# Sums of squares folded in transposed 32-blocks, factors kept as one row in memory, latents' factors spread by a product, gates run one group later

## The chip, the cores and the metric

The kernel runs on one core of a Trainium2 chip. The metric is device time in microseconds (us) of one execution. Engines are named as the profile names them: PE (TensorE, matmuls), DVE (VectorE), ACT (ScalarE), POOL (GpSimd) and SP (SyncE, which only issues DMAs here). PE, DVE, ACT and POOL each run their instructions strictly in the order in which the compiler lists them.

## The reference, cut to what matters

Two layers over 512 tokens and 2048 features, all in float32. One input projection feeds three mixers and a gate for each of their 16 heads; two places in the mixers divide by a root mean square over features, and these are what the change touches: the latents of the first mixer and the heads of the differential mixer.

```python
def rms_norm(x, g):
    y = x * lax.rsqrt(jnp.mean(x * x, axis=-1, keepdims=True) + NORM_EPS)
    return y * g

def mla_mixer(c_q, c_kv, k_rope, pos, q_norm_g, kv_norm_g, w_uq, w_ukv):
    q = (rms_norm(c_q, q_norm_g) @ w_uq)        # c_q: 384 features ("cq")
    kv = (rms_norm(c_kv, kv_norm_g) @ w_ukv)    # c_kv: 256 features ("ckv")
    ...
def diff_mixer(q, k, v, pos, lam, lam_init, subln_g):      # 5 heads of 128 features
    pr = softmax(q1 k1) - lam * softmax(q2 k2)
    o = rms_norm(pr @ v, subln_g) * (1.0 - lam_init)
    ...
for i in range(DEPTH):                                      # DEPTH = 2
    z = rms_norm(h, norm_g[i]) @ w_in[i]
    o_a, o_b, o_c = mla_mixer(...), dsa_mixer(...), diff_mixer(...)     # 6, 5 and 5 heads
    h = h + concat(o_a * silu(g_a), o_b * silu(g_b), o_c * silu(g_c)) @ w_o[i]
    h = h + (p[i] @ w_ple[i]) * sigmoid(h @ w_pg[i])
return rms_norm(h, final_g)
```

## The kernel before

Activations lie transposed: features on the 128 partitions, the 512 tokens on the free axis, one tile of 128x512 for each 128 features (pool name "g", 59 buffers, `slot()`). A float32 matrix product is made of two halves of each operand, high and low, in a type that TensorE takes at one column rate (`split_into`, L258: ACT copies the high half, L260, DVE subtracts it from the source, L261), and of three products (`mm3`, L356, lines L358 to L360).

**The input projection** runs through 15 groups (`IN_GROUPS`), each of up to four output tiles of 128 features. A group goes through 8 chunks of weights (DMA by SP into "wr", split into "wh" and "wl", 4 buffers each), with 24 matmuls a chunk, and sums in four accumulators in PSUM (pool "pp", 4 banks, so that the next group can begin only in those banks that have been emptied). When a group ends, `take` empties its banks: for queries and keys by an ACT copy (L633), for gates by a DVE product with the factors R (L629) and a silu on ACT (L630). What it writes to are "raw" tiles (pool name "z", 8 buffers for all).

**The mixers** run as a side stream (`mixers`): between two steps of the projection `pump` lets the stream go on by as much PE time as its share allows; a `yield` with a number books the PE time of what was just issued. `heads` runs first the five heads of the differential mixer (c0 to c4), then the five of the sparse mixer: scores (L364, L365), softmax (L547, L548 and behind them L815, L816), transposes of the probabilities (L564), their split into "th" and "tl" (L260, L261), the product with the values (the twelve matmuls of one `attend`), for c heads the squares of the result (L821), and a copy (L644) which POOL sends to memory (L646). A head's query and key raw tiles come free when `rope` has read them, which is done for the next head behind the one at hand.

The groups that the prediction speaks of: group 6 makes gates ga0, ga1 and qc1, kc1 (query and key of head c1); group 7 qc2, kc2, qc3, kc3; group 8 ga2, ga3, qc4, kc4; group 9 qb0, kb0, qb1, kb1; group 10 ga4, ga5, qb2, kb2; group 11 qb3, kb3, gc0, gc1; groups 12 to 14 hold the other gc and all gb gates.

**Norms.** `col_sums` (L308) turns the sum over the 128 partitions into four float32 matmuls with the data as weights and two columns of ones as the moving side (L313), so that each token's sum stands in a partition of its own; `rsqrt` works on these columns; `spread` (L330) brings them back, by four transposes of a broadcast column (L334), to a 128x512 tile whose rows are all alike. `latents` (L650) uses both (two calls a layer), `diff_after` (L825) sums for each c head into "csum", and `gate` (L900) spreads csum for each gc head.

**Gates.** At the end of each group the main loop (L949 to L953) takes all its tiles and then runs `gate` for its gates: load of the head's output from memory (SP, L905), product with the silu of the raw tile (DVE, L911 for ga and gb, L909 for gc). The raw tile of a gate is held until this product.

The scheduler places the instructions of all streams on their engines ahead of time; the list of each engine is fixed in the program.

Of the kernel before, what the change touches and what calls it, by code (L numbers as in the profile page):

```python
# [198 lines left out]
def trunk(ctx: ExitStack, tc: tile.TileContext, t, out):  # L199
# [53 lines left out]
    identb = const.tile([128, 128], BF16, name="identb")  # L253
    DVE.tensor_copy(identb, identf)
    onesf = const.tile([128, 2], F32, name="onesf")
    DVE.memset(onesf, 1.0)
# [47 lines left out]

    mean = const.tile([128, 4 * C_H], F32, name="mean")
    corr = const.tile([128, 4 * C_H], F32, name="corr")

# [7 lines left out]

    def rsqrt(dst, src, n, size):

        y, m, e = dst[:, :n], mean[:, :n], corr[:, :n]
        o = 0
        for x in src if isinstance(src, list) else [src]:  # L320
            DVE.tensor_scalar(mean[:, o:o + x.shape[1]], x, 1.0 / size, EPS, op0=ALU.mult, op1=ALU.add)
            o += x.shape[1]
        ACT.activation(y, m, AF.Sqrt)
        DVE.reciprocal(y, y)
        DVE.tensor_tensor(e, y, y, op=ALU.mult)
        DVE.tensor_tensor(e, e, m, op=ALU.mult)
        DVE.tensor_scalar(e, e, -0.5, 1.5, op0=ALU.mult, op1=ALU.add)
        DVE.tensor_tensor(y, y, e, op=ALU.mult)
# [256 lines left out]
    for L in range(DEPTH):  # L585
# [24 lines left out]
        def take(nm):  # L610
            nonlocal wi
            kind, j = nm
            if kind in ("vb", "vc", "v5"):
# [9 lines left out]
                if kind == "v5":  # L623
                    wi = const.tile([128, NB, 8], F32, name=f"wi{L}")
                    for b in range(NB):
                        DVE.tensor_scalar(wi[:, b], z[nm][b][:, 256:264], rcol[:, b:b + 1], None, op0=ALU.mult)
# [23 lines left out]
        def latents(kind, n, size, gain, res):  # L650
# [8 lines left out]
            yield GAP  # L659
            r = sm(4)  # L660
            rsqrt(r, col_sums(total), 4, size)
            yield 0.45
            yield GAP
            rb = spread(r)
            for j in range(n):
# [125 lines left out]

        csum = const.tile([128, 4 * C_H], F32, name=f"csum{L}")

# [31 lines left out]
        def diff_after(x, s):  # L825
            DVE.tensor_copy(csum[:, 4 * x:4 * x + 4], col_sums(s))
            yield 0.45
            if x == C_H - 1:
                rsqrt(csum, csum, 4 * C_H, 128)
                done.add(("csum", 0))  # L830

# [68 lines left out]
        def gate(kind, x):  # L900
            m = {"ga": 0, "gb": 6, "gc": 11}[kind] + x
            s = raw.pop((kind, x))
            finish(("out", m))
            o = slot()
            nc.sync.dma_start(o, odram[m])  # L905
            if kind == "gc":
                finish(("csum", 0))
                DVE.tensor_tensor(o, o, spread(csum[:, 4 * x:4 * x + 4]), op=ALU.mult)
                DVE.scalar_tensor_tensor(o, o, sub_c[:, L:L + 1], s, op0=ALU.mult, op1=ALU.mult)  # L909
            else:  # L910
                DVE.tensor_tensor(o, o, s, op=ALU.mult)  # L911
            gated[m] = o
# [11 lines left out]
        def mix(k):  # L924
            mix_until(k + 4)
            return mixed[k]

        fac = factors()
        main = Side(mixers(), SHARE)
        Side(choose(), 0.37)  # L930
        for gi, names in enumerate(IN_GROUPS):
# [4 lines left out]
            for got in gen:  # L936
                if gi == 0 and L == 0 and got == 2:
                    angles()
                if gi == 0 and L == 0 and got == 4:
                    lambdas()  # L940
                if gi == 0 and got in (5, 6):
                    next(fac)
                if gi == len(IN_GROUPS) - 1 and got in (3, 4, 5, 6):
                    mix_until(got - 2)
# [4 lines left out]
            for nm in names:  # L949
                take(nm)  # L950
            for nm in names:
                if nm[0] in ("ga", "gb", "gc"):
                    gate(*nm)  # L953
        if L == 0:
# [151 lines left out]
```

## Time and profile before

| what | us |
|---|---|
| median of 3 runs | 2294.86 (2294.57 to 2295.43) |
| the profiled execution | 2295.42 |
| its span in the trace | 2293.6 |
| PE busy | 2272.2 (99%) |
| DVE busy | 1366.9 (60%) |
| ACT busy | 1006.9 (44%) |
| POOL busy | 114.9 (5%) |

The mean granted clock of TensorE was 0.997 of full speed. The busy time of PE comes from ends that are modelled: a matmul overlaps the next one, so what one costs is read from the distance between two starts, not from its printed duration. Two more views are used: the timeline of an engine (start, duration, engine, line, operation, tiles, count, and in brackets the idle time ahead and what ended it) and a table of stretches of time with each engine's busy time and the granted clock.

### The profile page before, as it was taken

To read this page: it belongs to the slowest core of one execution; us is meant where nothing else is said; L and a number is where in the kernel's file an instruction comes from. 1 tells how busy PE (TensorE), PEld (TensorE's weight loads), DVE (VectorE), ACT (ScalarE), POOL (GpSimd) and SP (SyncE) were. 2 spreads that over 40 slices of the span, in tenths; PEclk is the share of its full clock that TensorE was granted. 3 is DMA by queue.
4 is the path that set the end of the run, shared out by engine and by line. 5 is a ranking of instruction groups with operands and counts; after the bars stand their busy time and mean duration, and the time that the engine had idled before them with its cause. 6 is when DMAs were issued, how large, how long until landed. Compare 5 with 4: busy or idle time off the path is not lost.

```text
span 2293.6 us, 29988 instructions
## 1 busy us (share of the span) xinstructions
PE 2272.2 (99%) x10988; PEld 1913.0 (83%) x10988; DVE 1366.9 (60%) x2886; ACT 1006.9 (44%) x1931; POOL 114.9 (5%) x204
## 2 busy tenths in 40 slices
PE   8999999999999999999999999999999999999997
PEld 7898888888888888888888888888888888888887
DVE  7655559977767543344555555699676665333445
ACT  6444445454545432233434444444554454223444
POOL 0000000000000011000000000000000000110003
PEclk9999999999999999999999999999999999999998
DMA  6233323323334345344332333233232243553235
GB/s 201 70 99 116 113 79 96 111 93 97 97 101 161 106 139 185 126 134 136 128 96 76 101 120 104 83 97 102 97 106 102 88 165 115 170 174 130 100 102 165
DMA packets 95220, 268.33 MB, mean 117 GB/s; under 512 B 10976, under 2 KB 26848, under 8 KB 95072
## 3 DMA queue, kind: packets, MB, share of 16 engines
q1 hardware_dynamic: 81760, 223.41, 30.5%
q0 software_dynamic: 13312, 43.00, 5.5%
q8 instruction: 86, 1.41, 0.3%
q14 instruction: 62, 0.51, 0.1%
HBM read 235.96 MB, written 30.41 MB: 116 GB/s over the span
## 4 chain that ended last, share of the span: by engine, by line
PE 98%; ACT 0%; issue 0%; DMA 0%; POOL 0%; SPq 0%; DVE 0%; POOLq 0%; ACTq 0%
PE pp L358 28%; PE pp L359 28%; PE pp L360 28%; PE at L360 3%; PE at L359 3%; PE at L358 3%; PE at L564 2%; PE at L365 1%; PE at L364 1%; PE at L313 1%; PE at L334 0%; DMA x<-in_x_dram 0%; PE at L853 0%; POOL g L1044 0%; ACT wh L260 0%
## 5 line engine op out<-in xcount | busy, mean ns | idle before, releaser
L261 DVE TENSOR_TENSOR wl<-wr,wh 128x512 fp32r<-128x512 f32 (+4 forms) x810 | 530.5, 660 | 731.4 <-ACT wh L260 671.2
L358 PE MATMUL pp<-g,wh 128*128 128x512 f32 (+1 forms) x2432 | 936.0, 386 | 6.2 <-ACT g L263 5.7
L359 PE MATMUL pp<-g,wh 128*128 128x512 f32 (+1 forms) x2432 | 936.1, 385 | 0.0
L260 ACT ACTIVATE wh<-wr 128x512 fp32r<-128x512 f32 (+4 forms) x810 | 487.1, 605 | 978.3 <-PE pp L359 723.9
L360 PE MATMUL pp<-g,wl 128*128 128x512 f32 (+1 forms) x2432 | 911.7, 386 | 0.0
L358 PEld LDWEIGHTS pp<-g,wh 128*128 128x128 f32 x2432 | 457.7, 188 | 94.1 <-ACT g L263 5.7
L359 PEld LDWEIGHTS pp<-g,wh 128*128 128x128 f32 x2432 | 457.6, 188 | 87.5
L360 PEld LDWEIGHTS pp<-g,wl 128*128 128x128 f32 x2432 | 456.7, 188 | 88.6
L359 PE MATMUL pp<-wl,g 128*128 128x512 f32 (+1 forms) x384 | 136.3, 357 | 0.0
L360 PE MATMUL pp<-wh,g 128*128 128x512 f32 (+1 forms) x384 | 135.7, 355 | 0.0
L358 PE MATMUL pp<-wh,g 128*128 128x512 f32 (+1 forms) x384 | 129.3, 363 | 1.2 <-ACT wh L260 1.2
L548 ACT ACTIVATE e<-at,sm 128x128 f32<-128x128 f32 (+3 forms) x128 | 67.0, 525 | 49.5 <-DVE sm L547 48.3
L358 PEld LDWEIGHTS pp<-wh,g 128*128 128x128 f32 x384 | 71.1, 188 | 11.5 <-ACT wh L260 2.1
L360 PEld LDWEIGHTS pp<-wh,g 128*128 128x128 f32 x384 | 72.2, 188 | 9.9
L359 PEld LDWEIGHTS pp<-wl,g 128*128 128x128 f32 x384 | 72.3, 188 | 9.1
L547 DVE TENSOR_REDUCE sm<-at 128x1 f32<-128x128 f32 (+3 forms) x168 | 77.2, 481 | 2.0
L646 POOL DMA_DIRECT2D o_d<-t x32 | 17.4, 542 | 1099.6 <-ACT t L644 1099.6
L261 DVE TENSOR_TENSOR tl<-at,th 128x512 fp32r<-128x512 f32 (+3 forms) x128 | 54.3, 483 | 16.8 <-ACT th L260 16.8
L365 PE MATMUL at<-g 128*128 128x512 f32 (+3 forms) x176 | 53.9, 324 | 0.0
L364 PE MATMUL at<-g 128*128 128x512 f32 (+3 forms) x176 | 53.7, 323 | 0.0
L260 ACT ACTIVATE th<-at 128x512 fp32r<-128x512 f32 (+3 forms) x128 | 45.5, 440 | 18.2 <-PE at L564 18.0
L564 PE MATMUL at<-identf,e 128*128 128x128 f32 x320 | 51.9, 273 | 0.0
(224 smaller groups left out, 2405.2 us busy)
## 6 DMA issues: line engine op xcount, KB each, us to landing
wr<-in_w_in_dram SPq DMA_DIRECT2D x207, 512.0 KB, 3.6
wr<-in_w_pg_dram SPq DMA_DIRECT2D x72, 512.0 KB, 3.7
wr<-in_w_o_dram SPq DMA_DIRECT2D x64, 512.0 KB, 3.7
o_d<-t POOLq DMA_DIRECT2D x32, 256.0 KB, 2.3
g<-o_d SPq DMA_DIRECT2D x32, 256.0 KB, 4.3
hm_d<-t POOLq DMA_DIRECT2D x32, 256.0 KB, 3.2
wr<-in_w_in_dram SPq DMA_DIRECT2D x18, 256.0 KB, 2.6
wr<-in_w_in_dram SPq DMA_DIRECT2D x16, 264.0 KB, 2.6
```

What stands on the lines that cost most here:

```text
L260: ACT.activation(hi, src, AF.Copy)
L261: DVE.tensor_tensor(lo, src, f32(hi), op=ALU.subtract)
L313: PE.matmul(ps[:, 2 * b:2 * b + 2], y[:, 128 * b:128 * b + 128], onesf, start=True, stop=True)
L358: PE.matmul(ps, l[0], r[0], start=start, stop=False)
L359: PE.matmul(ps, l[0], r[1], start=False, stop=False)
L360: PE.matmul(ps, l[1], r[0], start=False, stop=stop)
L364: PE.matmul(ps, q[:, qs], k[0][:, :n], start=start, stop=False)
L365: PE.matmul(ps, q[:, qs], k[1][:, :n], start=False, stop=stop)
L547: DVE.tensor_reduce(st[:, 1:2], ps[:, :n], op=ALU.max, axis=AX.X, negate=True)
L548: ACT.activation(e, ps[:, :n], AF.Exp, bias=st[:, 1:2], accum_out=st[:, 2:3])
L564: PE.transpose(ps[:, 128 * (i - kb):128 * (i - kb) + 128], probs[:, BO[i] + 128 * kb:BO[i] + 128 * kb + 128], identf)
L646: nc.gpsimd.dma_start(odram[m], o)
```

## The change

A sum of squares over partitions is now made by `fold`: DVE sums each row's blocks of 32 tokens with a transpose inside 32x32 blocks (the tile "part", 128x16), and one float32 matmul of 128x32 weights ("folded", four identity blocks on top of each other) adds the four partition groups, so that the 512 sums stand as 32 partitions x 16. `latents` takes its factors from there by `unfold`: DVE spreads the 32x16 factors into a 32x512 tile which is zero off the diagonals, and one float32 matmul with 32x128 ones makes the 128x512 tile. The c heads write their sums side by side into one tile (32x80, a `slot()`); behind the fifth, `rsqrt` works on all, DVE transposes them, and POOL writes them to memory as one row of 512 for each head ("row"); each gc gate reads its row into all 128 partitions by a POOL DMA (`head_norm`). `factors` keeps `col_sums` and `spread`. The tile `wi` comes from another pool. Gates are not run at the end of their group but at the sixth step of the next one (`got == 5`), those of the last group behind the loop.

```diff
+    folded = const.tile([128, 32], F32, name="folded")
+    DVE.tensor_reduce(folded, identf.rearrange("p (a j) -> p j a", j=32), op=ALU.add, axis=AX.X)
...
+    def fold(s):
+
+        part = small.tile([128, 16], F32, name="part", tag="part", bufs=2)
+        DVE.tensor_reduce(part, s.rearrange("p (b j) -> p b j", j=32), op=ALU.add, axis=AX.X, apply_transpose=True)
+        ps = at()
+        PE.matmul(ps[0:32, 0:16], folded, part, start=True, stop=True)
+        return ps[0:32, 0:16]
+
+    def unfold(r):
+
+        d = tmp()[0:32]
+        DVE.tensor_tensor(d.rearrange("p (b j) -> p b j", j=32), r.unsqueeze(2).to_broadcast([32, 16, 32]),
+                          identf[0:32, 0:32].unsqueeze(1).to_broadcast([32, 16, 32]), op=ALU.mult)
+        ps = at()
+        PE.matmul(ps, onesf[0:32, 0:1].to_broadcast([32, 128]), d, start=True, stop=True)
+        return ps
...
-            r = sm(4)
-            rsqrt(r, col_sums(total), 4, size)
-            yield 0.45
+            r = small.tile([32, 16], F32, name="part", tag="part", bufs=2)
+            rsqrt(r, fold(total), 16, size)
+            yield 0.25
             yield GAP
-            rb = spread(r)
+            rb = unfold(r)
...
         def diff_after(x, s):
-            DVE.tensor_copy(csum[:, 4 * x:4 * x + 4], col_sums(s))
-            yield 0.45
+            if x == 0:
+                norms["c"] = slot()
+                DVE.memset(norms["c"][0:32, 80:96], 0.0)
+            c = norms["c"][0:32]
+            DVE.tensor_copy(c[:, 16 * x:16 * x + 16], fold(s))
+            yield 0.25
             if x == C_H - 1:
-                rsqrt(csum, csum, 4 * C_H, 128)
-                done.add(("csum", 0))
+                rsqrt(c, c[:, 0:80], 80, 128, c[:, 96:176], c[:, 192:272])
+                DVE.transpose(c[:, 288:384], c[:, 0:96])
+                nc.gpsimd.dma_start(row_d.rearrange("a p j -> p a j"), c[:, 288:384].rearrange("p (a j) -> p a j", a=3))
+                done.add(("norm", 0))
+
+        def head_norm(x):
+
+            o = slot()
+            nc.gpsimd.dma_start(o, bass.AP(tensor=row_d.tensor, offset=row_d.offset + 512 * x, ap=[[0, 128], [1, 512]]))
+            return o
...
             if kind == "gc":
-                finish(("csum", 0))
-                DVE.tensor_tensor(o, o, spread(csum[:, 4 * x:4 * x + 4]), op=ALU.mult)
+                finish(("norm", 0))
+                DVE.tensor_tensor(o, o, head_norm(x), op=ALU.mult)
...
+        waiting = []
...
+                if got == 5:
+                    while waiting:
+                        gate(*waiting.pop(0))
...
-            for nm in names:
-                if nm[0] in ("ga", "gb", "gc"):
-                    gate(*nm)
+            waiting += [nm for nm in names if nm[0] in ("ga", "gb", "gc")]
+        for nm in waiting:
+            gate(*nm)
```

The lists of instructions change with it. The new kernel's line numbers stand some 2 lines higher at the top (L260 becomes L262), 20 higher from `mm3` on (L358 to L360 become L378 to L380) and 33 higher in `gate` (L911 becomes L944). In the rows below, a row is a line, an operation, the tile written and the tiles read, the shape and a count of equal instructions in a row.

ACT around the end of group 8, where head c1's softmax has ended, in the list of before: the two gates' silu, the copies "th" of c1's probabilities, and the two copies L633 that empty the banks of qc4 and kc4, one ahead of "th" and one ahead of the squares L821 of head c1.

```order
L630 ACTIVATE z<-z 128x512 x2
L633 ACTIVATE z<-pp 128x512
L260 ACTIVATE wh<-wr 128x512
L260 ACTIVATE th<-at 128x512
L260 ACTIVATE th<-at 128x384
L260 ACTIVATE th<-at 128x256
L260 ACTIVATE th<-at 128x128
L260 ACTIVATE wh<-wr 128x512
L633 ACTIVATE z<-pp 128x512
L821 ACTIVATE g<-at 128x512
L644 ACTIVATE t<-at 128x512
```

The same place in the list after:

```order
L650 ACTIVATE z<-z 128x512 x2
L262 ACTIVATE wh<-wr 128x512 x2
L262 ACTIVATE th<-at 128x512
L262 ACTIVATE th<-at 128x384
L262 ACTIVATE th<-at 128x256
L262 ACTIVATE th<-at 128x128
L842 ACTIVATE g<-at 128x512
L664 ACTIVATE t<-at 128x512
L653 ACTIVATE z<-pp 128x512 x2
```

Both copies of the banks (now L653) have moved behind the squares and the copy of head c1's result.

ACT around the end of group 10 in the list of before, with the two copies of the banks of qb2 and kb2 (L633) ahead of the first exponential of head c4 (L548):

```order
L260 ACTIVATE g<-v 128x512
L633 ACTIVATE z<-pp 128x512
L260 ACTIVATE wh<-wr 128x512
L630 ACT_TABLE_LOAD
L630 ACTIVATE z<-z 128x512
L260 ACTIVATE wh<-wr 128x512
L633 ACTIVATE z<-pp 128x512
L630 ACTIVATE z<-z 128x512
L548 ACT_TABLE_LOAD
L548 ACTIVATE e,sm<-at,sm 128x128
```

The same two copies in the list after, where head c4's exponentials (now L568) and all that follows from them come first:

```order
L568 ACTIVATE e,sm<-at,sm 128x512
L568 ACTIVATE t,sm<-at,sm 128x512
L262 ACTIVATE th<-at 128x512
L262 ACTIVATE th<-at 128x384
L262 ACTIVATE th<-at 128x256
L262 ACTIVATE th<-at 128x128
L842 ACTIVATE g<-at 128x512
L664 ACTIVATE t<-at 128x512
L653 ACTIVATE z<-pp 128x512 x2
L265 ACTIVATE g<-t 128x512
```

They have moved from ahead of the whole softmax of head c4 to behind its squares and its copy.

PE at head c4 in the list of before: from the sums of head c3 (L313) to the second batch of transposes (L564), with projection matmuls (pp) in between.

```order
L313 MATMUL at<-onesf,g 128x2 x4
L564 MATMUL at<-identf,e 128x128 x3
L360 MATMUL pp<-g,wl 128x512
L358 MATMUL pp<-g,wh 128x512
L359 MATMUL pp<-g,wh 128x512
L360 MATMUL pp<-g,wl 128x512
L358 MATMUL pp<-g,wh 128x512
L359 MATMUL pp<-g,wh 128x512
L564 MATMUL at<-identf,e 128x128 x3
```

PE at the same head in the list after, from the last scores (L384, L385) over the sum of head c3 (L323) and all ten transposes (L584) into the product with the values:

```order
L384 MATMUL at<-g 128x512
L385 MATMUL at<-g 128x512
L323 MATMUL at<-part,folded 32x16
L584 MATMUL at<-identf,e 128x128 x10
L378 MATMUL at<-th,g 128x512
L379 MATMUL at<-tl,g 128x512
L380 MATMUL at<-th,g 128x512
L378 MATMUL at<-th,g 128x384
L379 MATMUL at<-tl,g 128x384
```

No projection matmul is left between the last scores of the head and its last product with the values; the next one stands behind the twelfth of these. In the list of before 22 stand between the scores and L313 alone.

## Rows read from the trace of the kernel before

**Rows 1.** The page: engines' busy time, then the chain of waits by engine.

```profile
PE 2272.2 (99%) x10988; PEld 1913.0 (83%) x10988; DVE 1366.9 (60%) x2886; ACT 1006.9 (44%) x1931; POOL 114.9 (5%) x204
PE 98%; ACT 0%; issue 0%; DMA 0%; POOL 0%; SPq 0%; DVE 0%; POOLq 0%; ACTq 0%
```

**Rows 2.** Groups of PE by line: count | busy us, mean ns | idle before.

```profile
L313 PE MATMUL at<-onesf,g 128*128 128x2 f32 x112 | 13.3, 240 | 0.0
L334 PE MATMUL at<-identf,csum 128*128 128x128 f32 x40 | 5.8, 275 | 0.0
```

**Rows 3.** Timeline of PE (start, us, instruction) at the sums for the first latents.

```profile
67.21 0.39 PE L360 MATMUL pp<-g,wl 128*128 128x512 f32 x1
...
68.12 0.95 PE L313 MATMUL at<-onesf,g 128*128 128x2 f32 x8
68.93 0.49 PE L360 MATMUL pp<-g,wl 128*128 128x512 f32 x1
69.25 0.40 PE L359 MATMUL pp<-g,wh 128*128 128x512 f32 x1
```

**Rows 4.** Timeline of PE at the spreading of the first latents' factors.

```profile
75.42 0.60 PE L334 MATMUL at<-identf,sm 128*128 128x128 f32 x4
75.78 0.48 PE L359 MATMUL pp<-g,wh 128*128 128x512 f32 x1
76.09 0.40 PE L360 MATMUL pp<-g,wl 128*128 128x512 f32 x1
```

**Rows 5.** Timeline of PE in the group of values, at the second latents.

```profile
103.35 0.76 PE L358 MATMUL pp<-wh,g 128*128 128x264 f32 x4 [0.61 <-ACT wh L260]
```

**Rows 6.** Timeline of ACT from group 10's end to head c4's result.

```profile
582.90 0.58 ACT L633 ACTIVATE z<-pp 128x512 f32<-128x512 f32 x1
...
585.31 0.37 ACT L548 ACTIVATE e<-at,sm 128x128 f32<-128x128 f32 x1
...
599.22 1.43 ACT L260 ACTIVATE th<-at 128x512 fp32r<-128x512 f32 x4 [0.35 <-PE at L564]
...
606.87 0.60 ACT L821 ACTIVATE g<-at 128x512 f32<-128x512 f32 x1 [2.13 <-PE at L360]
607.37 0.59 ACT L644 ACTIVATE t<-at 128x512 f32<-128x512 f32 x1
```

**Rows 7.** Timeline of DVE over the same stretch.

```profile
579.55 1.28 DVE L629 TENSOR_TENSOR z<-pp,R 128x512 f32<-128x512 f32 x2
...
590.08 0.66 DVE L261 TENSOR_TENSOR wl<-wr,wh 128x512 fp32r<-128x512 f32 x1
...
594.43 0.75 DVE L816 SCALAR_TENSOR_TENSOR e<-e,sm,t 128x512 f32<-128x512 f32 x1
...
599.86 0.69 DVE L261 TENSOR_TENSOR tl<-at,th 128x512 fp32r<-128x512 f32 x1 [0.25 <-ACT th L260]
```

**Rows 8.** Timeline of PE: head c4's scores and its product with the values.

```profile
587.77 0.33 PE L364 MATMUL at<-g 128*128 128x384 f32 x1
...
589.17 0.39 PE L365 MATMUL at<-g 128*128 128x512 f32 x1
...
604.82 0.39 PE L358 MATMUL at<-th,g 128*128 128x512 f32 x1
...
606.56 0.27 PE L360 MATMUL at<-th,g 128*128 128x128 f32 x1
```

**Rows 9.** Timeline of PE at the kernel's start.

```profile
7.62 0.63 PE L359 MATMUL pp<-g,wh 128*128 128x512 f32 x1
8.05 0.63 PE L360 MATMUL pp<-g,wl 128*128 128x512 f32 x1
```

**Rows 10.** Stretches at the end: us; PE, PEld, DVE, ACT, POOL busy; granted clock, DMA share, GB/s.

```profile
2278.00:2280.00 2.00, 1.54 (x12) 1.46 (x12) 0.96 (x4) 1.25 (x4) 0.00 (x0) 1.00 0.00 0
2280.00:2282.00 2.00, 0.43 (x4) 0.32 (x3) 1.07 (x7) 0.20 (x1) 0.00 (x0) 0.63 0.00 0
```

**Rows 11.** The page's DMA issues: KB each, median us to landing.

```profile
posi<-in_positions_dram SPq DMA_DIRECT2D x1, 256.0 KB, 4.1
```

More of the change, by code (lines that the diff above doesn't have):

```diff
@@ L303, in add_square @@
             DVE.tensor_tensor(acc, acc, s, op=ALU.add)
-    mean = const.tile([128, 4 * C_H], F32, name="mean")
-    corr = const.tile([128, 4 * C_H], F32, name="corr")
+    mean4 = const.tile([128, 16], F32, name="mean")
+    corr4 = const.tile([128, 16], F32, name="corr")
     def col_sums(y):
@@ L314, in col_sums, with rsqrt @@
         return ps[:, 0:2 * nb:2]
-    def rsqrt(dst, src, n, size):
-        y, m, e = dst[:, :n], mean[:, :n], corr[:, :n]
+    def fold(s):
[11 more added lines that the diff above has]
+        return ps
+    def rsqrt(dst, src, n, size, mean=mean4, corr=corr4):
+        rows = slice(0, dst.shape[0])
+        y, m, e = dst[:, :n], mean[rows, :n], corr[rows, :n]
         o = 0
         for x in src if isinstance(src, list) else [src]:
-            DVE.tensor_scalar(mean[:, o:o + x.shape[1]], x, 1.0 / size, EPS, op0=ALU.mult, op1=ALU.add)
+            DVE.tensor_scalar(mean[rows, o:o + x.shape[1]], x, 1.0 / size, EPS, op0=ALU.mult, op1=ALU.add)
             o += x.shape[1]
@@ L623, in take @@
                 if kind == "v5":
-                    wi = const.tile([128, NB, 8], F32, name=f"wi{L}")
+                    wi = work.tile([128, NB, 8], F32, name="wi", tag="wi", bufs=1)
                     for b in range(NB):
@@ L789, in choose @@
             done.add(("bias", 0))
-        csum = const.tile([128, 4 * C_H], F32, name=f"csum{L}")
+        norms = {}
+        row_d = dram.tile([3, 32, 32], F32, name=f"row{L}", tag=f"row{L}")
         def diff_needs(x):
```

## The prediction

> **What bounds the kernel now.** I read the page first: PE is busy for 99% of the span, and the chain of waits is 98% PE [rows 1]. So time is saved only by taking work from PE, and lost wherever PE comes to stand still; DVE (60%) and ACT (44%) matter only where PE waits for them. Next I read PE's groups by line, for how much of the work the change removes, then the timeline of PE at single places for what such work costs as distance between starts, and at last the lists of instructions before and after for places where PE's next work has moved behind another engine's. The trace's own time is 2295.42 us, 0.56 above the median of the runs; I sum against it and take the 0.56 off at the end.
>
> **The unit.** From 67.21 to 68.12 PE starts four 512-column matmuls: 0.227 us each [rows 3]. This is the price of every full projection matmul here.
>
> **What is removed.** The sums: 112 records on L313 with a "g" tile as weights [rows 2]; the code gives 14 calls (2 latents and 5 heads in each of two layers) of four products, so each float32 product has two records. (`factors` sums another tile, "acc", and stays.) One call lies between 68.12 and 69.25, with one projection matmul among it: 1.13 - 0.23 = 0.90 us [rows 3]. 14 x 0.90 = 12.6. The spreading: from 75.42 to 76.09, again with one projection matmul, 0.67 - 0.23 = 0.44 for four transposes, 0.11 each [rows 4]. Ten calls for the gc gates (the 40 instructions of rows 2) and four for latents: 14 x 0.44 = 6.2. Together 18.8 us of PE work go, all on the path, since PE hardly ever waits.
>
> **What is added on PE.** `fold` is one float32 product with 32 columns of weights and 16 moving columns. The nearest row is the old sum's product, 0.90 / 4 = 0.23 [rows 3]; its moving side is as short, its weights four times as wide. Half of that if the narrow weights count: 0.11 to 0.23; I take 0.23, the row as it is. 14 x 0.23 = 3.2. By the Trainium skill ("TensorE: Matmul & The Clock Gate", section "LDWEIGHTS (loading the stationary operand)") the load time goes with the number of weight columns; that would put the fold at the low end, and the sum about 1 us lower. No row of this trace has weights of under 128 columns.
>
> `unfold` is a float32 product of 512 columns with weights of 32 partitions. No wide float32 product is in the trace. Nearest are the transposes: 128 float32 columns in 0.11, so 512 in 0.44 [rows 4], in one record each, where a float32 product has two [rows 2]. So 0.44 to 0.9; I take 0.9, as the product is the same kind as L313's. 4 x 0.9 = 3.6. The Trainium skill ("FP8 and Floating Point Precision", "TensorE Precision Notes") says that true FP32 takes four passes, high and low halves each with each. That speaks against this edit, since four passes of 512 columns cost twice what the four transposes did; the sum has this value in it already from the rows, and would be 1.8 us lower by the transposes' price.
>
> Net on PE: -18.8 + 3.2 + 3.6 = **-12.0**, with bounds of -9 (a fold at 0.45, twice the row) and -15.5 (both at their low ends).
>
> **What is added elsewhere.** On DVE a reduction of 128x512, a 32x512 product and small operations on 32 partitions; on POOL a row write and 5 row reads in each layer. DVE has 40% idle; the row reads are asked for well after the c heads have ended, and the trace's one load of the same kind, a row into all 128 partitions, takes 4.1 us [rows 11]. They delay a gate, which has the whole rest of the projection before w_o needs it. I put them at nothing; the cover is that no bank of PE's waits for a gc gate. wi's new place and the slot for the factors change nothing that I could find in PE's list.
>
> **What the moved gates do.** A gate's raw tile now stays until its product, one group later, and there are 8 raw tiles for everything. I looked in the lists for places where a bank of the projection is emptied behind work of a head, and found two in each layer.
>
> *A, end of group 8.* ga0, ga1 (put off), qc2, kc2, qc3, kc3, ga2 and ga3 are 8 tiles. The copies of qc4 and kc4 need qc2's and kc2's, so they stand behind head c1's whole result, in the list of ACT behind squares and copy; before, they stood ahead of the squares. PE has one round of 24 matmuls for the two free banks, then nothing until a bank is copied. The price from the same step at head c4: the product's last matmul starts at 606.56 (+0.11), the squares at 606.87, the copy at 607.37, and so the next ACT instruction at 607.86, its end 0.60 later, 608.46 [rows 6, 8]: 608.5 - 606.7 = **1.85 us** per layer.
>
> *B, end of group 10.* ga2 and ga3 still hold theirs, with qb0, kb0, qb1, kb1, ga4, ga5: 8 again. qb2's and kb2's copies now stand behind head c4's exponentials, splits, squares and copy. Before, the second of them ran at 582.90, ahead of the first exponential at 585.31 [rows 6]. So PE has for the whole of head c4 just 24 projection matmuls and the head's own work. The time: group 11 can begin when the first of ga4's and ga5's banks is emptied, half of L629's 1.28 after 579.55: 580.2 [rows 7]. The head's last DVE step ended at 594.43 + 0.75 = 595.18 [rows 7]; on its way lay three weight splits of 0.6 (one of them at 590.08), which no longer lie there, ACT comes 0.5 earlier without the copy of 582.90 (0.58 as printed, and it overlaps the next) [rows 6], and one small copy of 0.15 is new: 595.2 - 1.8 - 0.5 + 0.2 = 593.1. From there: the last four transposes of the ten and their way to ACT 0.4, the "th" copy 0.6, "tl" 0.7 behind it (599.22 to 599.86 to the next) [rows 6, 7]: product at 594.8. It takes 606.56 + 0.11 - 604.82 = 1.85 [rows 8]: 596.65. Then squares, copy, emptying as in A, 1.85: 598.5. In these 18.3 us PE has work for 24 x 0.227 = 5.45, eight scores 589.17 - 587.77 + 0.23 = 1.6 [rows 8], one fold 0.2, ten transposes 1.1 [rows 4], the product 1.85: 10.2. PE stands still for **8.1 us** per layer. Bounds: 6.5, if the denser head runs through DVE without the gaps it has now, and 9.5, if the transposes' splits wait for each other.
>
> *C, second latents.* Here PE already waits 0.61 for a weight split [rows 5]. The new list has three short waits in a row there, as unfold's work on DVE stands ahead of weight splits in a group whose matmuls are short. I take 0.65 more per layer, between 0 and 1.5 (the wait gone or twice more).
>
> **The clock.** While PE stands still its clock may fall. At the start, before PE has worked for long, 512-column matmuls are 0.43 apart [rows 9], which is the 1.2 GHz level against 0.227 at 2.4; and in the tail the granted clock of two stretches in a row is 1.00 and 0.63, the second where PE is busy for 0.43 of 2 us [rows 10]. In B PE has only transposes and a few scores for about 7.5 us (587 to 594.8). If the clock falls there, the product takes 1.85 more, and the first matmuls afterwards cost 0.2 more each until it rises: between 0 and 4 us per layer. I take 2.
>
> **Sum.** -12.0 + 2 x 0.65 (C) + 2 x 1.85 (A) + 2 x 8.1 (B) + 2 x 2 (clock) = +13.2. 2295.42 + 13.2 = 2308.6; less 0.56: **2308.0 us** as a median.
>
> **Rivals.**
>
> *Slower is wrong: the banks come free in time.* If raw tiles of ga2 and ga3 came free before head c4 (their products on DVE are only two instructions of 0.7), A and B would vanish and the saving stands alone: -12.0 + 1.3 = -10.7, 2284. The point from which it decides: with A as worked, C at 0.65 and no fall of the clock, the sum is zero where B costs (12.0 - 1.3 - 3.7) / 2 = 3.5 us. For it: a list says nothing of times, and PE is 99% busy now. Against: in the list the banks' copies stand behind the head's last product on a strictly ordered engine, so nothing can run earlier than that product. 8%.
>
> *No change: stalls without their clock, and cheap products.* Fold at 0.14 and unfold at 0.44 take 1.2 and 1.8 more off, -15.0; C 1.3, A 3.0, B 2 x 6.5 = 13.0: +2.3, less 0.56: 2297. For it: the short bounds all have a row. Against: all of them have to come together. 14%.
>
> *Slower by more: factor rows through memory.* Each gc gate waits on DVE for a row read behind others on POOL's queue, which is 4.1 us [rows 11]; the weight splits queued behind it on DVE would be late. PE holds 4 split halves in stock, about one chunk of 24 x 0.227 = 5.4 us, so one late row is hidden, and a second right behind it would cost 2 x 4.1 - 5.4 = 2.8 us in each layer: +5.6, 2313.6. For it: DVE stands still for the wait. Against: SP's loads of heads already end such waits now without any idle time on PE. 10%, beside the forecast on the same side.
>
> **How the numbers follow.** The forecast itself 68%, its spread 2299 to 2314 (B 6.5 to 9.5, clock 0 to 4, net products -9 to -15.5, not all at an end). With the rivals: faster by over 0.2% (below 2290.3) 8%; within 0.2% (what a measurement here can't tell from none; up to 2299.5) 14%; slower 78%. The range 2296 to 2316 takes in the forecast, the no-change case and the late rows, and leaves out the first rival and what is beyond.
>
> **What would show it.** In the changed kernel's trace: gaps of PE at the ends of groups 8 and 10 in both layers, ended by the banks' copies on ACT (now L653), about 2 and 8 us; no projection matmul between head c4's scores and its product; matmuls of 0.43 behind the gap if the clock fell. Sums on L323 at 0.11 to 0.23 of PE, L332 at 0.44 to 0.9, no L334 for gates. It is wrong if PE's idle time ahead of these copies is under 3 us, or if the gc gates' row reads end idle time on PE.

## The result and the profile after

The changed kernel takes 2312.37 us as a median of 4 runs (2311.78 to 2313.18), the kernel before on the same chip 2295.14 (2294.57 to 2295.8). The ratio is 1.0074 with a 95% interval of 1.0061 to 1.0086: slower, by some 17 us. The prediction was 2308.0, in a range of 2296 to 2316. The profiled span went from 2293.6 to 2310.0 us, +16.4.

The page of the changed kernel, busy time of the engines and the chain of waits by engine, to be read beside [rows 1]:

```profile
PE 2271.7 (98%) x10846; PEld 1901.8 (82%) x10856; DVE 1381.6 (60%) x2909; ACT 1005.6 (44%) x1929; POOL 121.1 (5%) x216
PE 77%; DVE 1%; ACT 0%; issue 0%; POOL 0%; POOLq 0%; ACTq 0%
```

PE has 142 matmul records fewer and is busy for the same time, since a part of its matmuls ran at a lower clock: with the same records and no fall of the clock before the tail it is busy for 2264.3 us, in the kernel with gates at their group's end (below). It has lost a point of its share of the span, and DVE has entered the chain. The shares of the chain add up to some 78% only, as the view follows it back no further than to the first copy of a bank at place A, at 487.18 us. The waits of PE (who waited <- for whom: us in total, times, longest) say where:

```profile
PE pp L378 <- ACT z L653: 6.7, 4, 1.7
...
PE at L584 <- DVE e L837: 4.4, 4, 1.6
PE pp L378 <- ACT wh L262: 3.1, 6, 0.9
PE at L378 <- DVE tl L263: 1.9, 2, 1.1
```

The first, second and last of these rows don't exist in the kernel before. The four waits for the copies of the banks (L653) are the two places A and B of the prediction, in two layers. Place A, timeline of PE, the last matmul of head c1's product and the first of the projection behind it:

```profile
485.79 0.27 PE L380 MATMUL at<-th,g 128*128 128x128 f32 x1
487.73 0.50 PE L378 MATMUL pp<-g,wh 128*128 128x512 f32 x1 [1.67 <-ACT z L653]
```

From start to start 1.94, of which 0.11 is the matmul: 1.83 us of standing still, and the same in the second layer. Place B in the first layer, timeline of PE from head c4's last score to the next projection matmul:

```profile
589.56 0.39 PE L385 MATMUL at<-g 128*128 128x512 f32 x1
590.48 0.23 PE L323 MATMUL at<-part,folded 128*32 128x16 f32 x2 [0.53 <-ACT e L568]
591.19 0.55 PE L584 MATMUL at<-identf,e 128*128 128x128 f32 x3 [0.47 <-ACT t L568]
593.38 0.90 PE L584 MATMUL at<-identf,e 128*128 128x128 f32 x3 [1.64 <-DVE e L837]
594.81 1.12 PE L584 MATMUL at<-identf,e 128*128 128x128 f32 x4 [0.53 <-DVE e L837]
596.70 0.80 PE L378 MATMUL at<-th,g 128*128 128x512 f32 x1 [0.77 <-DVE tl L263]
...
600.07 0.29 PE L380 MATMUL at<-th,g 128*128 128x128 f32 x1
602.02 0.50 PE L378 MATMUL pp<-g,wh 128*128 128x512 f32 x1 [1.66 <-ACT z L653]
```

Every step of the head waits here for the softmax on ACT and DVE, as no projection matmul is left to put between. The product takes from 596.70 to 600.07, 3.4 us to its last start, where it took 1.74 before [rows 8]. The table of stretches (us; PE, PEld, DVE, ACT, POOL busy; granted clock, DMA share, GB/s) tells why:

```profile
586.00:590.00 4.00, 3.95 (x19) 3.03 (x17) 3.01 (x12) 2.08 (x10) 0.00 (x0) 1.00 0.81 262
590.00:594.00 4.00, 1.40 (x8) 0.98 (x8) 3.78 (x13) 2.61 (x8) 0.00 (x0) 0.91 0.00 0
594.00:598.00 4.00, 2.69 (x9) 1.82 (x8) 2.79 (x7) 1.42 (x4) 0.00 (x0) 0.50 0.00 0
598.00:602.00 4.00, 2.36 (x10) 2.12 (x9) 3.06 (x7) 1.61 (x4) 0.23 (x1) 0.74 0.00 0
602.00:606.00 4.00, 3.98 (x17) 3.30 (x18) 3.90 (x7) 1.71 (x4) 0.31 (x1) 1.00 0.17 66
```

The granted clock goes from 1.00 over 0.91 to 0.50, the 1.2 GHz level, in and behind a stretch in which PE was busy for 1.40 of 4 us, and returns after the product. In the second layer it returned later, and the first projection matmuls were slow too:

```profile
1739.65 0.79 PE L378 MATMUL pp<-g,wh 128*128 128x512 f32 x1 [1.67 <-ACT z L653]
1740.24 0.63 PE L379 MATMUL pp<-g,wh 128*128 128x512 f32 x1
...
1743.61 0.39 PE L378 MATMUL pp<-g,wh 128*128 128x512 f32 x1
```

Nine matmuls from 1739.65 to 1743.61 took 3.96 instead of 2.04.

**The account.** B in the first layer: from the last score's end (589.56 + 0.23) to 602.02 are 12.23 us, in which PE at full clock has 0.2 (fold) + 1.1 (ten transposes) + 1.85 (product) = 3.15 to do: 9.1 lost. In the second layer, by the same two starts (1728.28 and 1739.65), 8.0, and 1.9 of slow matmuls behind: 9.9. A: 2 x 1.83 = 3.7. The latents' part, by the copies of the banks at the group ends before and behind it, costs 0.65 a layer: 1.3. The heads' sums and the gates' factors save 9.2 (worked out below). The end of the program takes 1.0 longer (below). -9.2 + 1.3 + 3.7 + 19.0 + 1.0 = +15.8 of the +16.4. Of the other 0.6 a wait of 0.24 for a weight split behind A in the second layer (1631.89), which the kernel before doesn't have, is a part; the rest I can't place.

### The profile page after: what moved, and what is told of

Same layout as the page of the kernel before. It is cut to its first block, busy times and chain, and to the rows that moved or that the text cites. A ratio compares the mean times of both kernels' runs of the same rounds, so it can differ in the third digit from the quotient of the medians.

```text
span 2310.0 us, 29768 instructions
## 1 busy us (share of the span) xinstructions
PE 2271.7 (98%) x10846; PEld 1901.8 (82%) x10856; DVE 1381.6 (60%) x2909; ACT 1005.6 (44%) x1929; POOL 121.1 (5%) x216
## 4 chain that ended last, share of the span: by engine, by line
PE 77%; DVE 1%; ACT 0%; issue 0%; POOL 0%; POOLq 0%; ACTq 0%
PE pp L378 22%; PE pp L379 22%; PE pp L380 22%; PE at L379 2%; PE at L380 2%; PE at L378 2%; PE at L584 1%; PE at L385 1%; PE at L384 1%; DVE sm L567 0%; POOL g L1081 0%; PE at L886 0%; DVE e L837 0%; ACT z L653 0%; PE at L332 0%
## 5 line engine op out<-in xcount | busy, mean ns | idle before, releaser
L378 PE MATMUL pp<-g,wh 128*128 128x512 f32 (+1 forms) x2432 | 938.3, 387 | 13.8 <-ACT z L653 6.7
L380 PE MATMUL pp<-g,wl 128*128 128x512 f32 (+1 forms) x2432 | 912.0, 386 | 0.0
L262 ACT ACTIVATE wh<-wr 128x512 fp32r<-128x512 f32 (+4 forms) x810 | 486.4, 605 | 958.1 <-PE pp L379 718.2
L378 PEld LDWEIGHTS pp<-g,wh 128*128 128x128 f32 x2432 | 458.3, 189 | 104.4 <-ACT z L653 7.3
L380 PEld LDWEIGHTS pp<-g,wl 128*128 128x128 f32 x2432 | 456.2, 188 | 87.8
L380 PE MATMUL pp<-wh,g 128*128 128x512 f32 (+1 forms) x384 | 135.3, 355 | 0.0
L378 PE MATMUL pp<-wh,g 128*128 128x512 f32 (+1 forms) x384 | 128.0, 363 | 1.9 <-ACT wh L262 1.9
L568 ACT ACTIVATE e<-at,sm 128x128 f32<-128x128 f32 (+3 forms) x128 | 66.9, 524 | 63.4 <-DVE sm L567 62.6
L380 PEld LDWEIGHTS pp<-wh,g 128*128 128x128 f32 x384 | 72.2, 188 | 9.8
L378 PEld LDWEIGHTS pp<-wh,g 128*128 128x128 f32 x384 | 70.1, 188 | 11.9 <-ACT wh L262 3.0
L584 PE MATMUL at<-identf,e 128*128 128x128 f32 x320 | 52.5, 276 | 5.2 <-DVE e L837 4.4
L262 ACT ACTIVATE th<-at 128x512 fp32r<-128x512 f32 (+3 forms) x128 | 45.6, 441 | 22.4 <-PE at L584 22.2
L385 PE MATMUL at<-g 128*128 128x512 f32 (+3 forms) x176 | 54.1, 325 | 0.0
L384 PE MATMUL at<-g 128*128 128x512 f32 (+3 forms) x176 | 53.5, 323 | 0.0
```

Source lines behind the costliest of these rows:

```text
L262: ACT.activation(hi, src, AF.Copy)
L378: PE.matmul(ps, l[0], r[0], start=start, stop=False)
L380: PE.matmul(ps, l[1], r[0], start=False, stop=stop)
L384: PE.matmul(ps, q[:, qs], k[0][:, :n], start=start, stop=False)
L385: PE.matmul(ps, q[:, qs], k[1][:, :n], start=False, stop=stop)
L568: ACT.activation(e, ps[:, :n], AF.Exp, bias=st[:, 1:2], accum_out=st[:, 2:3])
```

## The experiments

All medians below stand beside the kernel before on the same chip, 2295.7 to 2295.9 us in each of these sets (2295.14 beside the changed kernel above); kernels of different sets are compared as they stand.

**Gates at the end of their group again**, all else as changed:

```diff
-                if got == 5:
-                    while waiting:
-                        gate(*waiting.pop(0))
...
-            waiting += [nm for nm in names if nm[0] in ("ga", "gb", "gc")]
-        for nm in waiting:
-            gate(*nm)
+            for nm in names:
+                if nm[0] in ("ga", "gb", "gc"):
+                    gate(*nm)
```

> The changed kernel with one part undone: gates run at the end of their own group again, all else as changed. Theory (raw tiles held by the put-off gates cost some 22 us at the ends of groups 8 and 10; the smaller products save 8 to 9): both stalls go, no idle time on PE ahead of the banks' copies, 2286.8 us (2285 to 2289), faster than both. Rival 1 (the new sums and the factor rows themselves disturb head c4): the stall at head c4 stays in some form, 2300 or more. Rival 2 (the smaller products save nothing that counts): 2294 to 2296.

2289.03 us, ratio 0.9970 (0.9959 to 0.9982). Both stalls are gone; of PE's waits in the projection only the start's and the weight splits are left:

```profile
PE pp L378 <- ACT g L265: 6.0, 1, 6.0
PE pp L378 <- ACT wh L262: 1.9, 4, 0.5
```

So without the put-off gates the loss is gone, some 23 us, and the rest of the change is a gain. The gain is 6.7 where I expected 8.3, and 2289.03 lies on the upper edge of the range; the kernels with the heads' and the latents' part alone show where the rest went.

**The kernel before with only the gates put off** (the same edit the other way round on the old kernel):

> The kernel before with only the gates put off by a group; sums, factors and latents as before. Theory: PE stands still in head c4 of each layer, as in the changed kernel (9.1 and 9.7 us there with the lower clock), and not at the end of group 8, since the list of ACT keeps those two copies ahead of head c1's result here: 2295 + 18.7 = 2313.7 us (2309 to 2316). Rival 1 (it takes the new sums to make the stall): 2295.

2311.47 us, ratio 1.0066 (1.0051 to 1.0081). The stall in head c4 is there without any of the new sums, and there is none at the end of group 8: two waits for the copies (here L633), not four.

```profile
PE pp L358 <- ACT z L633: 3.3, 2, 1.7
```

The reason is not the one I had given. The copies stand behind head c1's result here too. Timeline of PE at the end of the head's product, then of ACT:

```profile
483.30 0.27 PE L360 MATMUL at<-th,g 128*128 128x128 f32 x1
483.41 0.45 PE L359 MATMUL pp<-g,wh 128*128 128x512 f32 x1
```

```profile
483.61 0.60 ACT L821 ACTIVATE g<-at 128x512 f32<-128x512 f32 x1 [4.35 <-PE at L360]
484.10 0.59 ACT L644 ACTIVATE t<-at 128x512 f32<-128x512 f32 x1
484.58 1.09 ACT L633 ACTIVATE z<-pp 128x512 f32<-128x512 f32 x2
```

The product ends 2.5 us earlier than in the changed kernel (483.30 against 485.79). Eleven projection matmuls are left behind it, and they last until the first bank is empty. "th" stands ahead of two weight splits in the list of ACT here and behind them in the changed kernel; what moved it there was not tried apart. So B needs only the put-off gates, while A needs them together with the rest of the change. The put-off gates cost 15.8 us here and 23.3 in the changed kernel; A's 3.7 are half of the difference.

Its four runs lie between 2308.1 us, at a mean granted clock of 0.996, and 2312.9 us, at 0.993.

**Ten raw tiles instead of eight**, gates put off as in the change:

```diff
-N_SLOTS = 59
-N_RAW = 8
+N_SLOTS = 57
+N_RAW = 10
```

> The changed kernel, gates put off as there, with 10 raw tiles instead of 8 and 57 other tiles instead of 59. Theory (it is the raw tiles that the put-off gates hold): both stalls go although the gates are late, 2286.8 us (2285 to 2290). Rival (the late gates cost by themselves: their loads and products on DVE fall where heads need DVE): the loss stays, 2308 to 2313.

2289.22 us, ratio 0.9971 (0.9959 to 0.9983), the time of the first kernel within 0.2. The gates are as late as in the changed kernel (the products of ga0 and ga2 on DVE at 489.90 and 613.52 us, there at 487.93 and 602.23) and cost nothing. So it is what they hold, not when they run: the raw tiles, at B those of ga2 and ga3. With these three runs the rivals by which the new sums, the factor rows or the lateness itself make the stall at B are out. At A the rest of the change has a part, but not without the held tiles.

**The heads' part alone**: gates at their group's end, latents as before.

```diff
-            r = small.tile([32, 16], F32, name="part", tag="part", bufs=2)
-            rsqrt(r, fold(total), 16, size)
-            yield 0.25
+            r = sm(4)
+            rsqrt(r, col_sums(total), 4, size)
+            yield 0.45
...
-            rb = unfold(r)
+            rb = spread(r)
```

> The changed kernel with gates at the end of their group and the latents' sums and factors as before: only the heads' sums by folding and their factors as rows in memory are left of the change. Theory, from starts in the changed kernel's trace: ten sums at 0.27 for 0.76 save 4.9, the gates' transposes 4.5, so 2295 - 9.4 = 2285.6 us (2284 to 2287), some 1 us under the kernel with the latents' part, which costs 1.43 for 1.34 in each of four calls and 0.35 more idle time per layer. Rival (the latents' part saves too, as the prediction had it by 0.2 each): 2288 or more, slower than the kernel with the latents' part.

2286.99 us, ratio 0.9962 (0.9947 to 0.9977), 2.0 faster than with the latents' part. So the latents' part is a loss. In the two traces 1.2 us of it lie ahead of the start of the last projection matmul, about what I had read from the starts (4 x 0.09 + 2 x 0.35); the other 0.8 lie behind it, where the granted clock fell to 0.50 at 2.7 us behind that start with the latents' part and at 4.3 us without.

**The latents' part alone**, on the kernel before (its rsqrt, fold and unfold; heads and gates as before):

> The kernel before with only the latents' part of the change: four calls of fold and unfold for sums and spreading; heads and gates as before. Theory, by starts in the changed kernel's trace: 0.27 + 1.16 for 0.90 + 0.44 in each call is +0.09, and 0.35 more idle time of PE per layer in the group of values: +1.1, 2296.6 us where before is 2295.5 (2296 to 2298). Rival (the prediction's term: fold 0.23, unfold 0.9, a saving of 0.2 a call, and 0.65 idle per layer): +0.5, 2296.0. By the kernel with heads and latents against that with heads alone, 2.0 slower: 2297.5.

2298.87 us, ratio 1.0012 (1.0002 to 1.0021): +3.1, above all three values that I had worked out. At the ends of the groups around the latents 0.65 a layer can be placed, 1.3 in all. In the profiled run (+3.6) 0.8 more lie in the tail, where the clock fell some us earlier than in the kernel before, and 1.5 are spread over later projections in steps of some 0.2 that I can't tie to the edit. That the latents' part costs is shown twice; its full size is not explained.

Why it costs shows where the starts are read from one matmul earlier. Timeline of PE in the changed kernel around a fold and around an unfold:

```profile
67.31 0.39 PE L380 MATMUL pp<-g,wl 128*128 128x512 f32 x1
67.63 0.23 PE L323 MATMUL at<-part,folded 128*32 128x16 f32 x2
67.79 0.50 PE L378 MATMUL pp<-g,wh 128*128 128x512 f32 x1
68.13 0.39 PE L379 MATMUL pp<-g,wh 128*128 128x512 f32 x1
...
75.18 0.39 PE L380 MATMUL pp<-g,wl 128*128 128x512 f32 x1
75.50 1.12 PE L332 MATMUL at<-t,onesf 32*128 32x512 f32 x2
76.55 0.50 PE L378 MATMUL pp<-g,wh 128*128 128x512 f32 x1
76.89 0.40 PE L379 MATMUL pp<-g,wh 128*128 128x512 f32 x1
```

The fold: 68.13 - 67.31 less two projection matmuls of 0.227 is 0.37, of which 0.09 lie ahead of it (67.63 - 67.31 - 0.23) and 0.11 behind the matmul that follows. The unfold: 76.89 - 75.18 - 0.45 = 1.26. The old sum and spreading, read in the same way, cost 69.25 - 67.89 - 0.45 = 0.91 and 76.09 - 75.19 - 0.45 = 0.45, with nothing ahead [rows 3, 4]; the matmuls ahead of them in the kernel before are:

```profile
67.89 0.39 PE L358 MATMUL pp<-g,wh 128*128 128x512 f32 x1
...
75.19 0.39 PE L358 MATMUL pp<-g,wh 128*128 128x512 f32 x1
```

So a latents' call went from 1.36 to 1.63.

**Unfold as two products of halves**, on the first kernel:

```diff
-        PE.matmul(ps, onesf[0:32, 0:1].to_broadcast([32, 128]), d, start=True, stop=True)
+        hi, lo = slot(F32R)[0:32], slot(F32R)[0:32]
+        split_into(hi, lo, d)
+        PE.matmul(ps, onesr[:, 0:1].to_broadcast([32, 128]), hi, start=True, stop=False)
+        PE.matmul(ps, onesr[:, 0:1].to_broadcast([32, 128]), lo, start=False, stop=True)
```

> The changed kernel with gates at the end of their group, and unfold's 32x512 tile split into a high and a low half, so that two products of ones with halves replace the one float32 product. Theory (unfold's 1.16 us is four passes of 512 columns): two products of 0.23 each take 0.7 off each of four calls, 2289.0 - 2.9 = 2286.1 us, at or below the kernel with the heads' part alone (2287.0). Rival (the split's steps on ACT and DVE make PE wait longer in the group of values): the 2.9 are given back in part, 2287.5 to 2289.

2288.91 us, ratio 0.9968 (0.9957 to 0.9980): nothing gained. Neither the theory nor the rival as written: the waits for weight splits are those of the first kernel, and each half costs nearly as much as three full matmuls. Timeline of PE around one:

```profile
75.60 0.39 PE L385 MATMUL pp<-g,wl 128*128 128x512 f32 x1
75.92 0.49 PE L336 MATMUL at<-g,onesr 32*128 32x512 f32 x1
76.34 0.50 PE L383 MATMUL pp<-g,wh 128*128 128x512 f32 x1
76.68 0.39 PE L384 MATMUL pp<-g,wh 128*128 128x512 f32 x1
```

76.68 - 75.60 - 0.45 = 0.63 for 512 columns that cost 0.23 with weights of 128 rows. The scheduler set the two halves apart, so this is paid twice, and 2 x 0.63 is just the 1.26 of the float32 product.

**PE kept busy in head c4.** The changed kernel with four matmuls of 384 columns ahead of each of head c4's four sets of transposes, whose result is overwritten:

```diff
+            for _ in range(idle):
+                PE.matmul(ps[:, 0:384], v(0)[0], v.whole[:, 0:384], start=True, stop=True)
             for i in range(kb, NB):
                 PE.transpose(...)
```

> The changed kernel with 16 matmuls of 384 columns added at head c4 of each layer, among its transposes, whose result is overwritten unread; the computation is unchanged. They cost 16 x 0.173 = 2.8 us of PE, most of it in time in which PE stands still. Theory (a part of the loss at head c4 is the lower clock): the clock stays up there, the product takes 1.85 instead of 3.6, and the matmuls behind it are at 0.227 at once: 4 to 6 us come back, less 1 to 3 for what isn't hidden: 2309 us (2307 to 2311). Rival (the clock falls all the same, or isn't what costs): 2313 to 2318.

2306.75 us, ratio 1.0047 (1.0032 to 1.0062): 5.6 us faster than the changed kernel, with 5.5 us more work on PE, and 0.25 below the range that I had given. The stretches of head c4:

```profile
590.00:594.00 4.00, 3.33 (x21) 3.16 (x22) 3.78 (x14) 2.32 (x8) 0.00 (x0) 1.00 0.00 0
594.00:598.00 4.00, 2.92 (x19) 2.40 (x18) 2.95 (x8) 1.43 (x4) 0.00 (x0) 1.00 0.00 0
598.00:602.00 4.00, 2.34 (x13) 1.87 (x12) 4.00 (x9) 2.07 (x4) 0.54 (x1) 1.00 0.17 66
```

The clock stays at 1.00, where it was 0.91, 0.50 and 0.74, and the product is back at 1.86 us from its first start at 596.27 to its last at 598.13. By the same starts as above 7.4 and 6.6 us are lost at B, where it was 9.1 and 9.9 (600.06 and 1736.17 for the first projection matmul, 589.27 and 1726.22 for the last score). So about 5 of the 19 us are the clock's, and the standing still that is left is some 7 us a layer.

**The factor rows on SP's queue**, on the heads' part alone (the row write and the five row reads of a layer):

```diff
-                nc.gpsimd.dma_start(row_d...
+                nc.sync.dma_start(row_d...
...
-            nc.gpsimd.dma_start(o, bass.AP(tensor=row_d.tensor, ...
+            nc.sync.dma_start(o, bass.AP(tensor=row_d.tensor, ...
```

> The kernel with the heads' part alone, with its row write and row reads issued by SP instead of POOL. Kernels with the row reads on POOL end 3.9 us after their last transfer, the one before and the one with put-off gates alone 3.0. If it is POOL's added transfers that lengthen the end: 2286.0 us, end 3.0. If it is the transfers as such, or their tile: 2287.0, end 3.9. If SP's queue, held by the row write, delays weights: more than 2287, with idle time of PE ahead of weight splits near head c4's end.

2285.81 us, ratio 0.9955 (0.9940 to 0.9970), 1.2 faster than with POOL. The last stretches with transfers in this kernel (span 2284.6) and, below, in the heads' part with POOL (span 2285.2):

```profile
2281.00:2282.00 1.00, 0.00 (x0) 0.00 (x0) 0.00 (x0) 0.00 (x0) 0.00 (x0) 0.50 0.66 226
```

```profile
2281.00:2282.00 1.00, 0.00 (x0) 0.00 (x0) 0.00 (x0) 0.00 (x0) 0.00 (x0) 0.50 0.28 93
```

By the shares the transfers end at about 2281.7 and 2281.3, the programs 2.9 and 3.9 us later. All traces bear it out: from the end of DVE's last step to the end of the program are 8.1 to 8.2 us in the six kernels with the rows on POOL, and 7.1 in the other seven, the one before among them. So the 1.0 at the end belongs to the transfers that POOL issues in addition. What the program does in that time the trace doesn't show. PE's waits for weight splits are 1.7 us in all, as in the kernel before, so SP's queue delayed none of them.

**A full-height product, wide weights, and both.** First unfold with the high half on partitions 0 to 31 of one tile, the low half on 32 to 63, zeros below, ones as 128x128 weights:

```diff
+        o = slot(F32R)
+        POOL.memset(f32(o)[64:128], 0.0)
+        ACT.activation(o[0:32], d, AF.Copy)
+        DVE.tensor_tensor(o[32:64], d, f32(o)[0:32], op=ALU.subtract)
         ps = at()
-        PE.matmul(ps, onesf[0:32, 0:1].to_broadcast([32, 128]), d, start=True, stop=True)
+        PE.matmul(ps, onesr[:, 0:1].to_broadcast([128, 128]), o, start=True, stop=True)
```

> The kernel with the heads' part and its rows on SP (2285.8 us), and the latents' part of the change again, but with unfold as one product of full height: high half of the 32x512 tile on partitions 0 to 31, low half on 32 to 63, zeros below, ones as weights. In the traces so far a product whose weights have 32 rows costs 0.63 us with 512 columns, where one with 128 rows costs 0.23; two such halves cost as much as the float32 product (1.26). Theory (the price is the small shape among full ones, not the passes): the product costs 0.23 to 0.3, the latents' part then saves 0.74 in the first and 0.2 in the second call of a layer (an idle time of 0.45 stays there): 2283.9 us (2283 to 2285). Rival (a float32 sum spread to all partitions costs its time whatever the shape): 2287 to 2288.

2283.66 us, ratio 0.9949 (0.9932 to 0.9965), as expected. One unfold now costs one matmul:

```profile
78.99 0.39 PE L385 MATMUL pp<-g,wh 128*128 128x512 f32 x1
79.22 0.40 PE L338 MATMUL at<-g,onesr 128*128 128x512 f32 x1
79.45 0.39 PE L386 MATMUL pp<-g,wl 128*128 128x512 f32 x1
```

Then fold with its 32 columns of weights written four times side by side (and one slot given up for them):

```diff
-        PE.matmul(ps[0:32, 0:16], folded, part, start=True, stop=True)
+        PE.matmul(ps[:, 0:16], wide, part, start=True, stop=True)
```

> The kernel with the heads' part and its rows on SP (2285.8 us), with fold's weights widened from 128x32 to 128x128, the same 32 columns four times. Theory (the small shape costs 0.09 ahead and 0.1 behind): the fold costs 0.2 to 0.3 instead of 0.37, so ten calls save 0.7 to 1.7: 2284.8 us (2284 to 2285.3). Rival (narrow weights load faster, so the narrow fold is the cheaper one): 2286 to 2287.

2285.41 us, ratio 0.9956 (0.9941 to 0.9971). This is 0.1 above the range of the theory and 0.6 below that of the rival. Against the kernel that it stands on it is 0.4, less than the scatter of both, so the time alone doesn't decide; the starts do:

```profile
470.64 0.39 PE L380 MATMUL pp<-g,wh 128*128 128x512 f32 x1
470.87 0.29 PE L324 MATMUL at<-part,wide 128*128 128x16 f32 x2
471.00 0.48 PE L381 MATMUL pp<-g,wl 128*128 128x512 f32 x1
471.32 0.40 PE L379 MATMUL pp<-g,wh 128*128 128x512 f32 x1
```

Nothing lies ahead of it, and it costs 471.32 - 470.64 - 0.45 = 0.23 instead of 0.37, though four times as many weights are loaded. From the start of the 97th projection matmul to that of the last, which leaves out what differs at the program's start and in its tail, the kernel is 0.9 us shorter (2235.3 against 2236.2), within the 0.7 to 1.7 of the theory.

> Both of these together: unfold of full height and wide fold weights, rows on SP, gates at the end of their group. Theory: 2285.8 - 1.9 - 1.4 = 2282.5 us (2281.5 to 2284.5), faster than every kernel so far. Rival (small shapes don't matter): 2287 to 2288.

2282.25 us, ratio 0.9940 (0.9925 to 0.9955), the fastest of all: 13.6 us under the kernel before, 30 under the changed one.

## Why the prediction was right, point by point

*A*, 1.85 per layer: 1.83 in both layers. The rows of the same step at another head gave the price; worked out without rounding they give 608.46 - 606.67 = 1.79. The list showed the place, but the order on ACT alone doesn't make the stall: with only the gates put off the copies stand behind the same result, and nothing waits, as PE has projection matmuls left. That none are left in the changed kernel the prediction took for granted, and it came out so.

*B*, 8.1 per layer and 2 for the clock: lost were 9.1 and 9.9; the run with PE kept busy puts the clock's part at 1.7 and 3.3 and the standing still at about 7, inside the bounds of 6.5 to 9.5 and 0 to 4. That the standing still came so near is in part luck, as two errors met. The head's product began at 596.7 instead of 594.8, because the last softmax step on DVE ended at 594.76, not at 593.1:

```profile
594.01 0.75 DVE L837 SCALAR_TENSOR_TENSOR e<-e,sm,t 128x512 f32<-128x512 f32 x1
```

I had moved the whole softmax forward by the weight splits that leave its way, but it starts from the scores, and the last of these started at 589.56, against 589.17 before [rows 8]. On the other side PE had more to do: from 580.2 on 31 projection matmuls, not 24, and eight more scores, of 128 columns each, some 2 us in all.

*C*, 0.65 more waiting per layer: 0.45 and 0.51, each with its 0.16 of ramp, in place of 0.61 [rows 5], so 0.35 more; two waits, not three.

*The products* were the mis-sized terms. The old sums were worth 4 x 0.91 + 10 x 0.84 = 12.0 (predicted 12.6; the heads' ones stood ahead of transposes and shared their ramp), the spreading 6.3 (6.2). But fold cost 0.37, not 0.23, and unfold 1.26, not 0.9: 5.2 + 5.0 instead of 3.2 + 3.6. The heads' part alone saves 10 x 0.84 + 4.5 - 10 x 0.37 = 9.2, and in the kernel with that part the last projection matmul starts 9.4 earlier than before, 4.7 from each layer. The step that failed was to take the price of a product with full weights for one with small weights, and to read it from the product's own start on. Read like [rows 3, 4], from their own starts, the two cost 0.27 and 1.16, and 0.1 more lies ahead of each. In the same place "about 1 us lower" for a fold at its low end should have been 14 x 0.12 = 1.7. The Trainium skill ("TensorE: Matmul & The Clock Gate", section "LDWEIGHTS (loading the stationary operand)") has the time of the load go with the number of weight columns. The trace agrees on the load itself, 108 ns for the 128x32 weights of the changed kernel and 188 ns for the 128x128 weights of the wide fold; but the load doesn't decide here, as the fold costs 0.37 with the former and 0.23 with the latter.

On unfold the Trainium skill ("FP8 and Floating Point Precision", section "TensorE Precision Notes") has four passes for true FP32. The trace fits that: the float32 product is 1.26 and the one-rate product of the same shape 0.63, so three more passes would be 0.63, 0.21 each, near the 0.227 of a full matmul.

*At nothing* I had put the row transfers, and on PE they were: no wait of PE has a row read at its end, and the third rival, late rows, didn't come. What I had not seen is the 1.0 at the program's end.

So the forecast came out 4 us low in the medians, and 3.2 in the profiled spans (+13.2 against +16.4), and the errors in part cancel. Too low were the products and C together by 2.8 (-10.7 against -9.2 + 1.3), the end by 1.0, and 0.6 is not placed; too high was B with its clock by 1.2 (20.2 against 19.0). Product by product, fold and unfold were 3.4 too cheap and the sums 0.6 too dear. The rival on the other side, 2284 with the banks free in time, is nearly what the kernel without put-off gates measures, 2289: it was ruled out by the order on ACT, and rightly, though at A that order alone would not have done it.

## What to carry to other kernels

When a consumer is put off, count the buffers it holds against all that is produced until it runs: the cost doesn't fall where the consumer stands but where a strictly ordered engine has to free a bank behind a chain that needs nothing of it. A saving of some us on the busiest engine is soon spent by one such place, and here the clock fell there too. Whether such a place costs anything depends on what work the waiting engine has left at that moment; an order of instructions alone doesn't tell it. And price a small matmul by four starts in a row, from the matmul ahead to the second behind; a shape that differs from its neighbours' can cost more than its columns.

## What the runs showed of the hardware

- Matmuls with weights of 32 rows or 32 columns among others of 128x128 had about 0.09 us ahead of them, which those with 128x128 weights had not, and 0.11 behind: 0.37 for a fold with 128x32 weights against 0.23 with 128x128, 0.63 for 512 columns under 32x128 weights against 0.23 under 128x128. Whether rows or columns alone do it, or the change of shape, was not tried apart.
- At head c4 the granted clock fell to 0.50 where PE was busy for 1.40 of 4 us, and it held at 1.00 where added matmuls brought that to 3.33; the added 5.5 us of work made the kernel 5.6 us faster.
- Twelve more transfers issued by POOL made the program end 1.0 us later: 8.1 to 8.2 us behind DVE's last step in the six kernels that have them, 7.1 in the other seven. Issued by SP they didn't.
